# The rwkv solves split by heads, one of the two within the keys' stage; earlier S5 loads; four gate blocks ahead of glu

## The chip, the cores and the metric

One core of one Trainium2 chip runs the program in one launch. The metric is the device time of one execution in microseconds (us); lower is better. All arithmetic is float32 in effect: each dense product is made of three matmuls of split operands (below).

## What is computed

One layer over 512 latent tokens x (width 1024) with a prefix ctx of 256 tokens, cut here to what matters:

```python
x = half_ffn(x, ...); ctx = half_ffn(ctx, ...)          # SwiGLU, 1024 -> 2816 -> 1024
proj = modulate(x) @ w_in                                # u | r k v | wd ad | gd | gate_a gate_b
ya = s5_scan forward + backward + s5_D * u               # 32 groups, 64 complex states, sequential in time
r, k, v = centred_conv(proj[r k v])                      # 3x3 depthwise over 8 rows of 64 tokens
yb = rwkv_scan forward + backward                        # 8 heads of 64, a state S of 64x64 per head:
#   sa = S @ aa;  S = S * w + outer(sa, bb) + outer(v, k);  y = S @ r
ya = gelu(ya); ya = ya * sigmoid(ya @ s5_w_glu)          # "glu"
yb = (groupnorm(yb) + bonus) * g @ rwkv_w_o              # "wo"
merged = sigmoid(gate_a) * (ya @ s5_w_proj) + sigmoid(gate_b) * yb
x = x + mod * (merged @ w_out); x = half_ffn(x, ...); return rmsnorm(x)
```

The scans of ctx come first and give the start states of those of x.

## The kernel before

**Dense work.** The weights are read in pieces of 512 KB (`raw`). ScalarE rounds each to `wh`, and VectorE or GpSimd (POOL) takes the rest `wl = raw - wh`; the activations are split likewise (`hx_109`, `hx_110` are the high and low part of x's). A product takes three matmuls for each tile: wh with high, wh with low, wl with high. A piece of `w_in` makes one or two blocks of 128 output channels by 512 tokens, 24 matmuls of 512 columns a block. The list `items` (in `build`, L400) names all dense work in order: the first FFNs, `w_in` for ctx and for x, `post_items` (L1916: glu, wo, proj, w_out), the second FFN. One generator, `dense` (L353), works it off. An item may carry names of events that it has to wait for.

**How the order is set.** A planner in Python (`Plan`, L53) runs while the program is written. Each piece of work is a generator that yields what it needs next (tiles, names of events, times); `run` (L165) takes the one of the lowest priority number whose needs are ready by the planner's own clock (`RATE`, `LAT`), and so fixes the order of the instructions on each engine. On the chip each engine, and SyncE's (SP's) queue of DMA issues, works strictly in that order and waits on semaphores.

**The keys' stage.** Beside the blocks of `w_in` for x (in the order wd, ad, k0 v0 r0 to k3 v3 r3, u0 to u3, gd, the 16 gate blocks) run `pb`, `pn`, `pa`, `conv` and `v_rows`. For each of four groups of key channels VectorE does the convolution (`cvk`, `cvr`, nine-tap products), a scan over the decays (`s`), and the products `kk`, `nb`, `ep`, `ks`, `st`, which end in `abk` (DMAs of `st`) and in `lf`: the triangular 32x32 matrices of each chunk of time, head and direction, written to DRAM (`pb`, L1430). `s5_in` (L1777) makes the inputs of the S5 scan from `u` and from `gt` tiles of `GTd`, 16 pairs, loaded one ahead; `s5_rec` (L1810) then does 63 steps of the S5 recurrence on POOL (`t`, `hs`).

**The solves.** `rw_solve(n)` (L1565) inverts the triangular matrices, 128 at a time, one on each partition. VectorE does 31 steps of a product (`prod`) and a sum (`Tl`) over a rectangle of (s + 1) x (31 - s), so 62 instructions; before them `AT` is read from `lf`, POOL writes the identity into `Tl` (affine_select), and behind them `Tl` and its transpose (`Tr`, by ScalarE) go to DRAM as `ti`. The eight heads come in four pairs j, as the groups of keys do. n = 0 is for ctx, chunks 0 to 3; n = 1 takes all heads of chunks 4 to 7 and n = 2 those of chunks 8 to 11, both in the next stage.

**Stage b2** (`phase_b2`, L1882). `rw_main` (L1704, priority 0) does the steps 4 to 11 of the rwkv scan, one for each chunk of time: PE products of `T` (read from `ti`), `M`, `Z` and `AB`; the last product of a step is b<-AB,Z. `rw_pre` (1) prepares the tiles, `solves` (1) does the two solves, `s5_out` (S5O = 2, L1830) waits for the event "s5recx", loads the first tiles and makes the outputs of the S5 scan in eight pieces (16 products U,Tz and 64 hs,gt each), `s5_post` (L2034) turns them into `yg`, and `rw_post(0)` finishes half 0 of the tokens. The gd and gate blocks (hx) fill PE between, a quota of columns at a time. `phase_c` (L2115) then does `rw_post(1)`, wo, proj, w_out and the second FFN. With `GLUP = 4` the two items of glu stand four gate blocks before the last of the gates.

Of the kernel before, what the change touches and what calls it, by code (L numbers as in the profile page):

```python
# [8 lines left out]
F32 = mybir.dt.float32  # L9
F32R = mybir.dt.float32r  # L10
AF = mybir.ActivationFunctionType
OP = mybir.AluOpType
# [31 lines left out]
GLUP = 4  # L44
# [240 lines left out]
class Kern:  # L285
# [114 lines left out]
    def build(self):  # L400
# [54 lines left out]
        self.items[i] += (["b2"],)  # L455
        self.n_post = len(self.items)
# [3 lines left out]
        self.w_slots(self.W, 2, 2)  # L460
        self.alt, self.dbanks = 0, (0, 5, 7)
        self.dn = self.dense()
        with ExitStack() as pb:
            hp = pb.enter_context(self.pool("hp"))
            X.h = self.hx = [hp.tile([128, KT, NX], F32R, name=f"hx{i}") for i in range(2)]
            self.bp = pb.enter_context(self.pool("bp", side="right"))
            bcs, self.bc = self.right("bc")
            self.phase_a()
            self.dbanks = (0, 5)
            self.s5s = ExitStack()  # L470
            X.sp = self.s5s.enter_context(self.pool("s5p"))
            X.hs = X.sp.tile([128, 65, 2, 32], F32, name="hs")
            sch = self.sch
            with self.pool("q") as X.q:
                self.phase_b1(X)
                sch.add(self.s5_in(X), 3)
                sch.add(self.s5_rec(X), 2)
                sch.run(self.ctxg, self.fill, *[sch.add(g(X), p) for p, g in self.b1_gens])
            self.wms.close()
            sch.run(sch.add(self.w_retire(self.wx), 0))  # L480
            self.wxs.close()
            bcs.close()
            self.dbanks = (0, 5)
# [946 lines left out]
    def pb(self, r):  # L1430
# [5 lines left out]
        for j in range(4):  # L1436
# [6 lines left out]
            for d in range(2):  # L1443
# [105 lines left out]
    def rw_setup(self, pool):  # L1549
# [13 lines left out]
        self.rwd, self.Ls = {}, {}  # L1563

    def rw_solve(self, n, sl):  # L1565

        nc = self.nc
        V, A_ = nc.vector, nc.scalar
        ti = self.dr.tile([2, 128, 32, 32], F32, name=f"ti{n}")
        tags = dict(tag="M", bufs=2) if n == 0 else {}  # L1570
        AT = sl.tile([128, 32, 32], F32, name="AT", **tags)
        nc.sync.dma_start(AT, self.lf[4 * n:4 * n + 4].rearrange("i c (a s) t -> (i c a) s t", s=32))
        Tt = sl.tile([128, 32, 32], F32, name="Tl", **tags)
        nc.gpsimd.affine_select(Tt, self.ones[:, 0:32][:, :, None].to_broadcast([128, 32, 32]),
                                pattern=[[1, 32], [-1, 32]], base=0, channel_multiplier=0,
                                compare_op=OP.is_equal, fill=0.0)
        yield [AT, Tt]
        pr = sl.tile([128, 32, 32], F32, name="prod", tag="bt" if n == 0 else "prod", bufs=2 if n == 0 else 1)
        w = 0
        for s in range(31):  # L1580
            o = (slice(None), slice(0, s + 1), slice(s + 1, 32))
            shape = [128, s + 1, 31 - s]
            V.tensor_mul(pr[o], Tt[:, :s + 1, s:s + 1].to_broadcast(shape), AT[:, s:s + 1, s + 1:32].to_broadcast(shape))
            V.tensor_add(Tt[o], Tt[o], pr[o])
# [7 lines left out]
        nc.sync.dma_start(ti[0], Tt)  # L1592
        nc.sync.dma_start(ti[1], Tr)
        for i in range(4):
            self.rwd[4 * n + i] = (ti, i)
        self.sch.post(f"solve{n}")
# [180 lines left out]
    def s5_in(self, r):  # L1777
# [10 lines left out]
        U, gts = self.s5_u(r, 0), [load(0)]  # L1788
        for t in range(4):
            Un = self.s5_u(r, t + 1) if t < 3 else None  # L1790
            for e in range(4):
                pr = t * 4 + e
                gt = gts.pop(0)
                if pr + 1 < 16:
                    gts.append(load(pr + 1))
# [34 lines left out]
    def s5_out(self):  # L1830
        nc, X, rw = self.nc, self.X, self.X.sp
        PE, A_ = nc.tensor, nc.scalar
        yield ["s5recx"]
# [12 lines left out]
        nxt, hts = load_t(0), [load(i) for i in range(HB - 2)]  # L1846
        for t in range(4):
# [34 lines left out]
    def phase_b2(self, pb):  # L1882
# [11 lines left out]
        def solves():  # L1894
            for n in (1, 2):
                yield from self.rw_solve(n, sv)
# [314 lines left out]
```

## Time and profile before

| what | value |
|---|---|
| runs | 1859.21, 1853.49, 1851.22 us; median 1853.49 |
| profiled execution, its own time | 1853.32 us |
| its span from first to last instruction | 1851.6 us |
| TensorE (PE) busy | 1688.9 us, 91% |
| VectorE (DVE) busy | 975.9 us, 53% |
| ScalarE (ACT) busy | 718.6 us, 39% |
| GpSimd (POOL) busy | 637.0 us, 34% |
| chain that ended last | PE 68%, DMA 10%, DVE 9%, ACT 5% |

The shares are means over stages with different limits. In the rows further down, a row of the timeline gives start, duration, engine, operation, output <- inputs, sizes and count, and in brackets the idle time before it with what ended that; the name of a tile stands without its buffer number. Nearly every instruction is issued in one helper, so that L210 stands for all of them, and the tiles' names tell them apart.

### The profile page before, as it was taken

The page shows a single profiled execution, that of the slowest core. Times are in us where ns is not written, and L with a number is a line of the kernel's source. Part 1 is how long each engine was busy: PE and PEld are TensorE (multiplying, and loading weights), DVE is VectorE, ACT ScalarE, POOL GpSimd, SP SyncE. Part 2 cuts the span into 40 slices and gives each one's busy share as a digit, 9 for nine tenths or more (in the row PEclk, how much of TensorE's full clock was granted, in tenths as well). Part 3 has the DMA queues.
Part 4 walks back from the last instruction along what each step waited for, and adds up shares of the span by engine and source line. Part 5 has one row for each costly group of instructions (what it writes and reads, how often), then busy time and mean ns, then how long its engine had stood idle before and what let it go on. Part 6 is the DMA issues. An engine that isn't in the chain of part 4 may idle for free.

```text
span 1851.6 us, 33250 instructions
## 1 busy us (share of the span) xinstructions
PE 1688.9 (91%) x13280; PEld 1402.9 (76%) x13280; DVE 975.9 (53%) x1733; ACT 718.6 (39%) x1200; POOL 637.0 (34%) x815
## 2 busy tenths in 40 slices
PE   7999999899899979978999889969799999999996
PEld 3699987778787857866557567758689988888886
DVE  3486564755666645554567655743366623323335
ACT  3355442444553214534444424443543432222221
POOL 0144231556676625621112127930124421111111
PEclk9999999999999989987989979989899999999998
DMA  8955541335355556434663666456464222332321
GB/s 327 344 171 194 186 148 59 115 113 163 106 145 159 155 160 192 132 114 137 208 205 111 193 201 191 141 158 181 147 213 149 69 92 91 102 102 91 103 91 58
DMA packets 207979, 278.44 MB, mean 150 GB/s; under 512 B 93617, under 2 KB 149937, under 8 KB 206801
## 3 DMA queue, kind: packets, MB, share of 16 engines
q1 hardware_dynamic: 207824, 276.32, 48.1%
q8 instruction: 105, 1.72, 0.4%
q14 instruction: 50, 0.40, 0.1%
HBM read 234.31 MB, written 43.22 MB: 150 GB/s over the span
## 4 chain that ended last, share of the span: by engine, by line
PE 68%; DMA 10%; DVE 9%; ACT 5%; issue 3%; POOL 3%; SPq 2%; DVEq 0%; ACTq 0%; POOLq 0%
PE b L210 68%; DMA wmod<-in_wmod 2%; SPq L210 2%; DMA raw<-in_win 2%; ACT wh L210 2%; DVE wl L210 1%; POOL t L210 1%; DMA gt<-GTd 1%; DVE rs L210 1%; DMA raw<-in_wgu 1%; DMA abk<-st 1%; DVE st L210 1%; DMA gt<-gates 1%; DMA AB<-abk 1%; ACT L210 1%
## 5 line engine op out<-in xcount | busy, mean ns | idle before, releaser
L210 PE MATMUL b<-hx,wh 128*128 128x512 f32 (+1 forms) x2432 | 698.5, 374 | 27.8 <-DVE x L210 12.4
L210 POOL TENSOR_TENSOR wl<-raw,wh 128x1024 fp32r<-128x1024 f32 x109 | 265.6, 2438 | 807.1 <-ACT wh L210 744.6
L210 PEld LDWEIGHTS b<-hx,wh 128*128 128x128 f32 x2432 | 437.0, 194 | 109.6 <-ACT wh L210 24.8
L210 PE MATMUL b<-hx,wl 128*128 128x512 f32 (+1 forms) x1216 | 447.8, 368 | 8.7 <-POOL wl L210 7.6
L210 DVE TENSOR_TENSOR wl<-raw,wh 128x1024 fp32r<-128x1024 f32 x164 | 226.9, 1384 | 293.8 <-ACT wh L210 291.2
L210 ACT CAST wh<-raw 128x1024 fp32r<-128x1024 f32 x273 | 283.1, 1046 | 195.7 <-DMA raw<-in_wgu 63.3
L210 PEld LDWEIGHTS b<-hx,wl 128*128 128x128 f32 x1216 | 235.0, 193 | 49.1 <-POOL wl L210 10.5
L210 PE MATMUL b<-ah,wh 128*128 128x512 f32 (+1 forms) x560 | 196.6, 351 | 2.4 <-ACT wh L210 1.5
L210 PE MATMUL b<-ah,wl 128*128 128x512 f32 (+1 forms) x560 | 194.2, 347 | 2.5 <-POOL wl L210 1.9
L210 PE MATMUL b<-al,wh 128*128 128x512 f32 (+1 forms) x560 | 194.3, 347 | 0.1
L210 PE MATMUL b<-hc,wh 128*128 128x256 f32 x928 | 173.2, 288 | 2.0 <-ACT hc L210 1.2
L210 PEld LDWEIGHTS b<-hc,wh 128*128 128x128 f32 x928 | 145.9, 193 | 13.1 <-issue 9.5
L210 PE MATMUL b<-hc,wl 128*128 128x256 f32 x464 | 131.5, 283 | 0.0
L210 PEld LDWEIGHTS b<-ah,wl 128*128 128x128 f32 x560 | 107.0, 191 | 16.2 <-POOL wl L210 2.1
L210 PEld LDWEIGHTS b<-ah,wh 128*128 128x128 f32 x560 | 106.9, 191 | 15.8 <-ACT wh L210 1.9
L210 PEld LDWEIGHTS b<-al,wh 128*128 128x128 f32 x560 | 107.0, 191 | 12.6 <-DVE al L210 0.5
L210 ACT CAST ah<-prod 128x512 fp32r<-128x512 f32 (+1 forms) x68 | 36.6, 538 | 204.5 <-DVE prod L210 204.3
L210 DVE TENSOR_TENSOR prod<-sil,b 128x512 f32<-128x512 f32 (+1 forms) x68 | 39.6, 583 | 107.3 <-PE b L210 89.2
L210 ACT ACTIVATE sil<-b 128x512 f32<-128x512 f32 (+1 forms) x68 | 35.0, 515 | 148.5 <-PE b L210 148.4
L210 PEld LDWEIGHTS b<-hc,wl 128*128 128x128 f32 x464 | 89.2, 192 | 0.0
L210 DVE SCALAR_TENSOR_TENSOR x1c<-b,gp,x1c 128x512 f32<-128x512 f32 (+1 forms) x67 | 43.9, 662 | 74.4 <-PE b L210 74.4
L210 DVE TENSOR_TENSOR al<-prod,ah 128x512 fp32r<-128x512 f32 (+1 forms) x68 | 43.1, 633 | 41.9 <-ACT ah L210 41.9
(297 smaller groups left out, 2327.9 us busy)
## 6 DMA issues: line engine op xcount, KB each, us to landing
raw<-in_wgu SPq DMA_DIRECT2D x132, 512.0 KB, 3.6
wmod<-in_wmod SPq DMA_DIRECT2D x72, 512.0 KB, 4.9
raw<-in_wdn SPq DMA_DIRECT2D x66, 512.0 KB, 3.7
raw<-in_win SPq DMA_DIRECT2D x49, 512.0 KB, 4.1
gt<-GTd SPq DMA_DIRECT2D x32, 256.0 KB, 3.6
abk<-st SPq DMA_DIRECT2D x8, 1024.0 KB, 6.1
AB<-abk SPq DMA_DIRECT2D x8, 1024.0 KB, 6.8
GTd<-gst SPq DMA_DIRECT2D x16, 256.0 KB, 2.4
```

The source lines that it names most:

```text
L210: r = f(out, *args, **kw)
```

## The change

1. `rw_solve(1)` now takes the pairs of heads j = 0 and 1 of all chunks 4 to 11, and runs as a generator `rw_early` (priority 3) within the keys' stage, as soon as "gp2" and "lfx3" (the fourth `lf` of x written) are there; `rw_solve(2)` takes the pairs 2 and 3 of the same chunks, in b2, once "lfx7" is there. Both write one `ti`, and "solve1" and "solve2" are posted after the second. `AT` is read, and `ti` written, by two DMAs each in place of one.
2. The identity is written by two memsets of VectorE in place of POOL's affine_select; `prod` is packed (128x256).
3. `s5_in` loads its `gt` three pairs ahead in place of one; `s5_out` issues its first loads (Tz, U, two gt of Hd) once "s5inx" and "b2" are there, ahead of its wait for "s5recx".
4. `GLUP = 0` puts the two glu items behind all gate blocks, and the fourth gate block from the end waits for the event "step11", which `rw_main` posts behind its last step.

```diff
-GLUP = 4
+GLUP = 0
...
         self.items[i] += (["b2"],)
+        self.items[-4] += (["step11"],)
...
-                sch.run(self.ctxg, self.fill, *[sch.add(g(X), p) for p, g in self.b1_gens])
+                early = sch.add(self.rw_early(), 3)
+                sch.run(self.ctxg, self.fill, early, *[sch.add(g(X), p) for p, g in self.b1_gens])
...
                 nc.sync.dma_start(self.lf[ps, d * 4 + j].rearrange("s p t -> p s t"), a1)
+                self.sch.post(f"lf{e_}{i}")
...
-        ti = self.dr.tile([2, 128, 32, 32], F32, name=f"ti{n}")
+        if n < 2:
+            self.ti = self.dr.tile([2, 32 * (4 if n == 0 else 8), 32, 32], F32, name=f"ti{n}")
+        ti = self.ti
+        def rows(t, d):
+            return t.rearrange("(i d j r) s t -> d i (j r) (s t)", d=2, j=4, r=4)[d, :, 8 * n - 8:8 * n]
...
-        nc.sync.dma_start(AT, self.lf[4 * n:4 * n + 4].rearrange("i c (a s) t -> (i c a) s t", s=32))
+        if n == 0:
+            nc.sync.dma_start(AT, self.lf[0:4].rearrange("i c (a s) t -> (i c a) s t", s=32))
+        for d in range(2 if n else 0):
+            nc.sync.dma_start(AT[d * 64:d * 64 + 64].rearrange("p s t -> p (s t)"),
+                              rows(self.lf[4:12].rearrange("i c (a s) t -> (i c a) s t", s=32), d))
...
-        nc.gpsimd.affine_select(Tt, self.ones[:, 0:32][:, :, None].to_broadcast([128, 32, 32]),
-                                pattern=[[1, 32], [-1, 32]], base=0, channel_multiplier=0,
-                                compare_op=OP.is_equal, fill=0.0)
+        V.memset(Tt, 0.0)
+        V.memset(Tt.rearrange("p a b -> p (a b)")[:, ::33], 1.0)
...
-        nc.sync.dma_start(ti[0], Tt)
-        nc.sync.dma_start(ti[1], Tr)
-        for i in range(4):
-            self.rwd[4 * n + i] = (ti, i)
-        self.sch.post(f"solve{n}")
+        for k, t in enumerate((Tt, Tr)):
+            if n == 0:
+                nc.sync.dma_start(ti[k], t)
+            for d in range(2 if n else 0):
+                nc.sync.dma_start(rows(ti[k], d), t[d * 64:d * 64 + 64].rearrange("p s t -> p (s t)"))
+        for p in {0: range(4), 1: (), 2: range(4, 12)}[n]:
+            self.rwd[p] = (ti, p % 4 if n == 0 else p - 4)
+            self.sch.post(f"solve{p // 4}")
+
+    def rw_early(self):
+        yield ["gp2", "lfx3"]
+        self.wms.close()
+        es, sl = self.right("sva")
+        yield from self.rw_solve(1, sl)
+        es.close()
...
-        U, gts = self.s5_u(r, 0), [load(0)]
+        ahead = 1 if r.v else HB - 1
+        U, gts = self.s5_u(r, 0), [load(i) for i in range(ahead)]
...
-        yield ["s5recx"]
+        yield ["s5inx", "b2"]
...
         nxt, hts = load_t(0), [load(i) for i in range(HB - 2)]
+        yield ["s5recx"]
...
-            for n in (1, 2):
-                yield from self.rw_solve(n, sv)
+            yield ["lfx7"]
+            yield from self.rw_solve(2, sv)
```

**VectorE in the keys' stage.** Before, behind the product `ks` and the scan `s` of the second group of keys, stand one weight split and then the convolution of the third (the nine taps `cvk`):

```order
L210 TENSOR_TENSOR ks<-cvv,b_10225 128x512
L210 SCALAR_TENSOR_TENSOR s_9125<-m_982,s_9125 128x520
L210 TENSOR_TENSOR wl<-raw,wh 128x1024
L210 SCALAR_TENSOR_TENSOR cvk<-pad_9121,cw,cvk 128x7x63
L210 SCALAR_TENSOR_TENSOR cvk<-pad_9121,cw,cvk 128x8x63 x2
```

In the changed kernel the early solve stands there, behind the same two:

```order
L210 TENSOR_TENSOR ks<-cvv,b_10237 128x512
L210 SCALAR_TENSOR_TENSOR s_9126<-m_982,s_9126 128x520
L210 TENSOR_TENSOR prod<-Tl,AT 128x31
L210 TENSOR_TENSOR Tl<-Tl,prod 128x31
L210 TENSOR_TENSOR prod<-Tl,AT 128x60
L210 TENSOR_TENSOR Tl<-Tl,prod 128x2x30
L210 TENSOR_TENSOR wl<-raw,wh 128x1024
L210 TENSOR_TENSOR prod<-Tl,AT 128x87
```

and after its 62 instructions, with that one weight split among them, the rest of the same convolution:

```order
L210 TENSOR_TENSOR prod<-Tl,AT 128x60
L210 TENSOR_TENSOR Tl<-Tl,prod 128x30x2
L210 TENSOR_TENSOR prod<-Tl,AT 128x31
L210 TENSOR_TENSOR Tl<-Tl,prod 128x31
L210 SCALAR_TENSOR_TENSOR cvk<-pad_9122,cw,cvk 128x7x63
L210 SCALAR_TENSOR_TENSOR cvk<-pad_9122,cw,cvk 128x8x63 x2
```

The third group's convolution (all but two of its `cvk`), and all that VectorE does for the third and fourth group behind it, now follows a whole solve; two further weight splits of that stretch stand on POOL.

**PE behind step 11.** Before, the last S5 output piece is still to come behind step 11, then the transposes of `s5_post` (ident,sg), two products of the g gate, and glu (yg), whose first rows are these:

```order
L210 MATMUL b_14036<-hs,gt 64x64
L210 MATMUL b_14080<-ident,sg_13978 128x128 x4
L210 MATMUL b_14103<-sgd,g_10991 128x256 x2
L210 MATMUL b_14155<-yg_14097,wh 128x512
L210 MATMUL b_14155<-yg_14098,wh 128x512
L210 MATMUL b_14155<-yg_14097,wl 128x512
```

In the changed kernel the last S5 piece stands ahead of step 11's last products, and gate blocks (hx) follow them:

```order
L210 MATMUL b_14007<-hs,gt 64x64
L210 MATMUL b_14051<-M,Z_13626 64x64 x16
L210 MATMUL b_14051<-AB,Z_13625 64x64 x16
L210 MATMUL b_14092<-hx_109,wh 128x512
L210 MATMUL b_14092<-hx_110,wh 128x512
L210 MATMUL b_14092<-hx_109,wl 128x512
```

96 matmuls of gate blocks stand now between step 11 and glu, and none between glu and wo; two of the eight S5 pieces have moved from behind step 11 to before its end. Between the ends of steps 4 and 11 there are 96 dense matmuls where there were 123.

**SP at the S5 loads of the x stage.** Before:

```order
L210 DMA udx<-gst 128x8x64
L210 DMA U<-udx 128x512
L210 DMA gt<-GTd 128x512
L210 DMA U<-udx 128x512
L210 DMA gt<-GTd 128x512
L210 DMA abk<-st 128x8x256
L210 DMA lf<-a_10835 128x8x32
```

and in the changed kernel:

```order
L210 DMA udx<-gst 128x8x64
L210 DMA U<-udx 128x512
L210 DMA gt<-GTd 128x512 x3
L210 DMA U<-udx 128x512
L210 DMA gt<-GTd 128x512
L210 DMA abk<-st 128x8x256
L210 DMA lf<-a_10921 128x8x32
```

Two more `gt` loads of 256 KB stand ahead of an `abk` and an `lf` of the fourth group of keys.

## Rows read from the trace of the kernel before

**Rows 1.** Windows: us, busy of each engine (x instructions), granted PE clock, DMA share, GB/s.
```profile
985.00:1054.00 69.00, 67.98 (x438) 49.15 (x439) 53.68 (x88) 31.10 (x46) 12.82 (x13) 1.00 0.46 130
994.00:1076.00 82.00, 68.65 (x594) 50.98 (x593) 57.32 (x93) 33.29 (x55) 14.33 (x19) 0.91 0.54 158
1140.00:1214.00 74.00, 69.63 (x1167) 56.08 (x1165) 50.31 (x91) 34.82 (x66) 67.01 (x180) 1.00 0.55 153
1214.00:1240.00 26.00, 11.97 (x233) 10.68 (x232) 9.02 (x22) 8.63 (x15) 4.58 (x13) 0.67 0.60 177
```

**Rows 2.** Waits of PE from 1054 to 1415: total us, times, longest us.
```profile
PE b L210 <- DMA T<-ti: 13.4, 2, 12.3
PE b L210 <- DMA gt<-GTd: 12.1, 5, 5.2
PE b L210 <- ACT yg L210: 7.8, 2, 7.1
```

**Rows 3.** Waits of DVE from 994 to 1076, by the same columns.
```profile
DVE st L210 <- DMA abk<-st: 6.1, 1, 6.1
...
DVE rs L210 <- PE b L210: 3.3, 2, 2.2
DVE nb L210 <- DMA bond<-ks: 2.0, 1, 2.0
```

**Rows 4.** DVE timeline: keys' stage, and two rows in the solve for ctx.
```profile
699.91 2.47 DVE L210 TENSOR_TENSOR Tl<-Tl,prod 128x252 f32<-128x252 f32 x1
702.41 0.42 DVE L210 TENSOR_TENSOR prod<-Tl,AT 128x247 f32<-128x247 f32 x1
...
988.40 1.23 DVE L210 TENSOR_TENSOR wl<-raw,wh 128x1024 fp32r<-128x1024 f32 x1 [0.97 <-ACT wh L210]
989.55 4.38 DVE L210 SCALAR_TENSOR_TENSOR cvk<-pad,cw,cvk 128x441 f32<-128x441 f32 x6
...
1075.27 0.69 DVE L210 TENSOR_TENSOR ks<-cvv,b 128x512 f32<-128x512 f32 x1 [4.67 <-PE b L210]
```

**Rows 5.** The fourth lf of x in SP's timeline; then all lf and AT DMAs.
```profile
978.90 0.36 SPq L210 DMA_DIRECT2D lf<-a  x1
DMA to landing us min/median/max: 1.8/4.7/9.0
```

**Rows 6.** Groups of DVE, three solves together: busy us, mean ns, idle before.
```profile
L210 DVE TENSOR_TENSOR Tl<-Tl,prod 128x31 f32<-128x31 f32 (+15 forms) x93 | 36.8, 396 | 3.2
L210 DVE TENSOR_TENSOR prod<-Tl,AT 128x31 f32<-128x31 f32 (+15 forms) x93 | 34.9, 376 | 2.8
```

**Rows 7.** PE timeline: first product of steps 4 and 8, last of step 11.
```profile
1139.83 0.89 PE L210 MATMUL b<-T,M 32*32 32x32 f32 x32
1226.36 0.28 PE L210 MATMUL b<-T,M 32*32 32x32 f32 x2 [12.33 <-DMA T<-ti]
1292.54 1.15 PE L210 MATMUL b<-AB,Z 64*64 64x64 f32 x32
```

**Rows 8.** PE timeline behind step 11: last S5 piece, glu, gate blocks, wo.
```profile
1301.17 0.69 PE L210 MATMUL b<-U,Tz 128*64 128x64 f32 x16 [0.78 <-DVE y L210]
1301.79 2.51 PE L210 MATMUL b<-hs,gt 64*64 64x64 f32 x64
1313.51 1.58 PE L210 MATMUL b<-yg,wh 128*128 128x512 f32 x2 [7.11 <-ACT yg L210]
1330.46 1.03 PE L210 MATMUL b<-sgd,g 128*128 128x256 f32 x4
1332.86 0.81 PE L210 MATMUL b<-hx,wh 128*128 128x512 f32 x2
1356.32 0.61 PE L210 MATMUL b<-hx,wh 128*128 128x512 f32 x2
1357.00 0.61 PE L210 MATMUL b<-hx,wh 128*128 128x512 f32 x2
1357.69 1.89 PE L210 MATMUL b<-sgd,g 128*128 128x256 f32 x8
1359.23 0.59 PE L210 MATMUL b<-yb,wh 128*128 128x256 f32 x2
```

**Rows 9.** POOL: the S5 recurrence (ns min/median/max, first and last start us); the affine_select.
```profile
L210 POOL TENSOR_TENSOR t<-t,hs x63: 312/322/1362, 1105.8 to 1218.4; 128x64 f32<-128x64 f32 x63
1133.92 1.26 POOL L210 TENSOR_SCALAR_AFFINE_SELECT Tl<-ones 128x1024 f32<-128x1024 f32 x1 [6.33 <-DMA ti<-Tl]
```

More of the change, by code (lines that the diff above doesn't have):

```diff
@@ L460, in build @@
         self.w_slots(self.W, 2, 2)
+        self.rwd = {}
         self.alt, self.dbanks = 0, (0, 5, 7)
@@ L1562, in rw_setup @@
                 nc.gpsimd.memset(t[q * 64 + 32:q * 64 + 64, :, 0:32], 0.0)
-        self.rwd, self.Ls = {}, {}
+        self.Ls = {}
     def rw_solve(self, n, sl):
@@ L1568, in rw_solve @@
         V, A_ = nc.vector, nc.scalar
-        ti = self.dr.tile([2, 128, 32, 32], F32, name=f"ti{n}")
+        if n < 2:
+            self.ti = self.dr.tile([2, 32 * (4 if n == 0 else 8), 32, 32], F32, name=f"ti{n}")
+        ti = self.ti
         tags = dict(tag="M", bufs=2) if n == 0 else {}
+        def rows(t, d):
+            return t.rearrange("(i d j r) s t -> d i (j r) (s t)", d=2, j=4, r=4)[d, :, 8 * n - 8:8 * n]
         AT = sl.tile([128, 32, 32], F32, name="AT", **tags)
-        nc.sync.dma_start(AT, self.lf[4 * n:4 * n + 4].rearrange("i c (a s) t -> (i c a) s t", s=32))
+        if n == 0:
[3 more added lines that the diff above has]
+                              rows(self.lf[4:12].rearrange("i c (a s) t -> (i c a) s t", s=32), d))
         Tt = sl.tile([128, 32, 32], F32, name="Tl", **tags)
-        nc.gpsimd.affine_select(Tt, self.ones[:, 0:32][:, :, None].to_broadcast([128, 32, 32]),
-                                pattern=[[1, 32], [-1, 32]], base=0, channel_multiplier=0,
-                                compare_op=OP.is_equal, fill=0.0)
+        V.memset(Tt, 0.0)
+        V.memset(Tt.rearrange("p a b -> p (a b)")[:, ::33], 1.0)
         yield [AT, Tt]
-        pr = sl.tile([128, 32, 32], F32, name="prod", tag="bt" if n == 0 else "prod", bufs=2 if n == 0 else 1)
+        pr = sl.tile([128, 256], F32, name="prod", **(dict(tag="w") if n == 0 else {}))
         w = 0
@@ L1582, in rw_solve @@
             shape = [128, s + 1, 31 - s]
-            V.tensor_mul(pr[o], Tt[:, :s + 1, s:s + 1].to_broadcast(shape), AT[:, s:s + 1, s + 1:32].to_broadcast(shape))
-            V.tensor_add(Tt[o], Tt[o], pr[o])
+            q = pr[:, :(s + 1) * (31 - s)].rearrange("p (a b) -> p a b", b=31 - s)
+            V.tensor_mul(q, Tt[:, :s + 1, s:s + 1].to_broadcast(shape), AT[:, s:s + 1, s + 1:32].to_broadcast(shape))
+            V.tensor_add(Tt[o], Tt[o], q)
             w += 400 + 2.1 * (s + 1) * (31 - s)
@@ L1793, in s5_in @@
                 gt = gts.pop(0)
-                if pr + 1 < 16:
-                    gts.append(load(pr + 1))
+                if pr + ahead < 16:
+                    gts.append(load(pr + ahead))
                 yield [U, gt]
```

## The prediction

> **What bounds the kernel now.** I read the busy shares by stage first, then the waits of PE, then the timelines at the places that the change touches. Over the span PE is busy 91% of the time, so a gain can come only from stretches in which PE waits or is clocked down. In the keys' stage PE is full: 67.98 of 69 us at the full clock [rows 1]. Its last dense block ends shortly before 1054, and then PE waits for what VectorE (DVE) still has to do for the last group of keys: the stage ends with `ks` at 1075.27 [rows 4]. So from 994 on DVE's chain sets the end of that stage, though DVE is busy only 57.32 of the 82 us up to 1076 [rows 1]. In b2 PE is again nearly full from 1140 to 1214, the steps 4 to 7, and then stops once for 12.3 us, for the second solve's `T` [rows 2, 7]; behind that stop the granted clock averages 0.67 from 1214 to 1240 [rows 1]. Behind step 11 it stops for 7.1 us for `yg` [rows 2, 8].
>
> **The sum, against the profiled execution's 1853.3 us.** The median of the runs is 0.2 us from that, so the two need no correction.
>
> *1. The early solve on DVE: +21.* The three solves together take 36.8 + 34.9 us busy and 6.0 idle between their instructions [rows 6], so one takes 25.9. Its input is the fourth `lf`, issued at 978.90; that and the reading of `AT` take about 4.7 us each to land [rows 5], so the solve starts at about 988.3, where DVE has just become free. One weight split stands in it (1.23, [rows 4]), and two stand on POOL meanwhile. While POOL worked, one `Tl` of the ctx solve took 2.47 us where its neighbour took 0.42 [rows 4], so I add 2 x 2.05. Then follow the third group's taps, 4.38 [rows 4]. Together 988.3 + 25.9 + 1.2 + 4.1 + 4.4 = 1023.9, where the taps ended at 993.93 before: the chain of the last two groups starts 30 us later. Of the 82 us to the end of the stage DVE idled 24.7 [rows 1]. 10.8 of these are the round trips at its very end, 6.1 for `abk` and 4.67 for PE [rows 3, 4], and stay. The other 13.9 can take up delay at most, so the stage ends between 16 and 30 us later. Of them 5.3 are waits that the chain brings with it (`rs` 3.3, `nb` 2.0, [rows 3]); I take the remaining 8.6 as absorbed, which gives 21. The packed `prod` and the memsets change nothing that a row shows; the memsets stand in front of the solve, while it waits for `AT`. SP's queue stands behind the `lf` until `AT` may be read, some 4.7 us; the weight pieces behind it are loaded ahead and cover that, and if they did not, PE would lose up to those 4.7 us, which lies within the bounds here.
>
> *2. Clock in the keys' stage: +2 (0 to 8).* PE now waits longer for DVE. The nearest row is that of 1214 to 1240: an average of 0.67 means some 17 of 26 us at 1.2 GHz [rows 1], and the wait itself covers up to 12.3 of them. So the work loses from 2.4 us, where the low clock covers the whole wait, to 8, where it covers none; some of it falls on work that waits for DVE anyway, so 2.
>
> *3. The `gt` loads of `s5_in`, three ahead: 0 (-12.1 to +2).* PE waited 12.1 us for them in five waits [rows 2], all beside the DVE chain that ends the stage, which now is longer still: the cover grows. Two loads more stand ahead of `abk` and `lf` on SP. The bound of -12.1 holds only where DVE isn't last, which the term before excludes; +2 is two more issues and their share of the traffic.
>
> *4. From the start of b2 to step 4: +1 (0 to 5).* One solve of the same size still stands there, with `AT` and `ti` in two DMAs each; its Tl identity leaves POOL.
>
> *5. Steps 4 to 11: -17.* They take from 1139.83 to 1293.69, or 153.9 us [rows 7]. Step 8 no longer waits for `T`: -13.4 in two waits [rows 2]. The low clock behind the stop goes too: between 2.4 and 8 as above, 4 taken. 27 fewer dense matmuls stand between: three take 0.68 us (from 1356.32 to 1357.00, [rows 8]), so -6.1. Two S5 pieces more stand there, each from 1301.17 to 1304.30, so 3.1 [rows 8]: +6.2. Bounds -8 (another wait keeps half) to -22.
>
> *6. From step 11 to wo and behind: -18.* The two S5 pieces leave (-6.2). 96 gate matmuls now stand over the chain that makes `yg`, 7.8 us of waits [rows 2]: -7.8. Glu ran from 1313.51 to 1330.46, 17 us, for 48 matmuls that take 10.9 at the full clock: -6. The gate blocks behind it ran 24.8 us (1332.86 to 1357.69, [rows 8]) where the full clock gives 21.8: -3. Against that, nothing now covers the chain behind glu and `rw_post` for wo: between nothing and another 7.1, the wait for `yg`, which is a chain of the same make; 5 taken. Bounds -13 to -24.
>
> Sum: +21 + 2 + 0 + 1 - 17 - 18 = -11, which gives 1853.3 - 11 = **1842**.
>
> **The rivals.**
>
> *A. The steps are not shortened, because the S5 recurrence on POOL comes late.* In the new order a piece of S5 output stands before the end of step 8, and PE waits in order. The recurrence starts when `s5_in` is done: 1105.8 before, some 21 later now, and took 113 us to 1218.8 [rows 9]. Without the affine_select and the wait for it (1.26 + 6.33, [rows 9]) it takes 105.4 and ends at about 1232. Step 8 begins at 1139.83 + 24 + 74 = 1238. The margin is 6 us. For it: POOL was 67 of 74 us busy in b2 [rows 1]. Against it: 250 operations of 0.32 us need only 81 us [rows 9], and the rest of the 113 is waiting, part of it beside a solve that is gone. If the recurrence is 17 us late, PE loses the 11 beyond the margin: 1842 + 11 = **1853**. Chance 0.22.
>
> *B. The delay is absorbed.* The planner may have used the 13.9 us of DVE's idle time wholly, and POOL may not hold the solve: 30 - 13.9 - 4.1 = 12, and no clock loss: 1842 - 9 - 2 = **1831**. Chance 0.12.
>
> *C. Slower: PE loses its clock in the keys' stage itself.* The products that need the third group's taps stand among dense blocks that PE does in order. If PE gets there before DVE, it stops within the dense work, not behind it, and then runs its dense matmuls at 1.2 GHz. In the 69 us of rows 1 PE ran at 2.4 GHz without a gap; 32 us of that work at half clock cost 32 us more, and the DVE chain does not hide this, since the last group's taps wait for those blocks. It decides from the point where the stage's delay exceeds 21 + 11 + 9 = 41 us; with 32 of loss, of which 3 are already counted, the time is 1842 + 29 = **1871**. For it: the drop to 0.67 behind one stop of 12.3 us. Against it: dense blocks stand between the solve and those products (some 40 to 53 dense matmuls were moved in ahead of them, 9 to 12 us). The Trainium skill ("TensorE: Matmul & The Clock Gate", Part 1: The HAM clock gate) calls the throttled clock the default state, which activity releases; by that rule a stop in mid-stage would bring 1.2 GHz with it, as in C, and the trace agrees, with 0.67 behind the stop. Chance 0.09.
>
> *D. The early solve is not early.* If its `AT` landed only with the last `lf`, both solves would follow each other in b2 and step 4 would wait for both: the 12.3 us stop returns ahead of step 4, and only term 6 is left: 1853 - 18 + 12 = 1847. The `lf` at 978.90 speaks against it. Chance 0.05.
>
> **How the numbers follow.** The forecast has 0.52, and its own range is 1829 to 1853, from the bounds: the keys' stage 5 less or 9 more, terms 5 and 6 some 9 either way, not all at once. Rival B lies in it, and A just at its end; C lies outside. 0.08 is left out on the slow side and some 0.1 below 1827, so the range is 1827 to 1857. A measurement of this kernel tells 0.5%, 9.3 us, from no change: faster is below 1844.2, slower above 1862.8. Faster: 0.41 of the forecast's 0.52, 0.12 of B, and 0.02 of D: 0.55. Slower: C's 0.09. The rest, 0.36, is within.
>
> **What would show it.** Right: 62 solve instructions on DVE from about 988 to 1018; the stage's last `ks` at about 1096; no wait of PE for `ti` behind step 4's; steps 4 to 11 in about 137 us at a clock of 1.00; no wait of over 2 us for `yg`; glu in 11 us; a new wait of some 5 us ahead of wo. Wrong: a PE wait for `hs` or Hd within steps 8 to 11 (A); a last `ks` before 1088 (B); a granted clock well under 1.00 before the last dense block of the keys' stage (C); the gain of term 6 eaten by a wait for `yb` of over 10 us.

## The result, and the profile after

Median of the changed kernel 1868.2 us (1862.0 to 1872.5), of the kernel before, measured beside it, 1855.7; ratio 1.0067, 95% interval 1.0038 to 1.0096. It is about 12 us slower where 11 us faster were forecast, and outside the range of 1827 to 1857. The profiled execution took 1870.22 us, with a span of 1868.4. From the page: the busy row of PE and the chain that ended last, by engine.

```profile
PE 1699.7 (91%) x13280; PEld 1416.2 (76%) x13280; DVE 974.1 (52%) x1735; ACT 721.0 (39%) x1202; POOL 642.7 (34%) x816
...
PE 61%; DVE 12%; DMA 11%; ACT 5%; POOL 5%; issue 4%; SPq 2%; DVEq 0%; ACTq 0%; POOLq 0%
```

PE's share of the chain falls from 68% to 61%, and what waits on DVE, DMA and POOL takes its place. The windows, by the columns of [rows 1], for the keys' stage, two stretches of the steps and the stretch from step 11 to w_out; the second and third hold earlier steps than in [rows 1], as step 4 now begins 31 us later:

```profile
985.00:1054.00 69.00, 53.86 (x313) 36.78 (x312) 58.44 (x118) 23.27 (x34) 12.58 (x9) 0.88 0.30 94
1140.00:1214.00 74.00, 68.34 (x708) 54.28 (x706) 32.88 (x54) 28.93 (x47) 66.95 (x180) 0.95 0.52 148
1214.00:1240.00 26.00, 23.65 (x466) 20.00 (x466) 9.97 (x16) 13.07 (x27) 12.57 (x43) 1.00 0.61 159
1319.50:1429.70 110.20, 95.04 (x580) 84.69 (x581) 64.82 (x104) 53.95 (x77) 37.21 (x16) 0.95 0.62 199
```

The stretch from step 11 to w_out in the kernel before:

```profile
1293.70:1414.40 120.70, 105.72 (x760) 93.34 (x761) 69.89 (x119) 54.33 (x83) 30.21 (x13) 0.90 0.59 191
```

In the keys' stage PE is busy 53.86 of 69 us where it was 67.98 [rows 1], at a clock of 0.88 instead of 1.00. The DVE timeline there, answering to [rows 4]:

```profile
988.90 0.19 DVE L210 TENSOR_TENSOR prod<-Tl,AT 128x31 f32<-128x31 f32 x1 [0.75 <-DMA AT<-lf]
...
1001.59 2.48 DVE L210 TENSOR_TENSOR Tl<-Tl,prod 128x256 f32<-128x256 f32 x1
...
1015.10 0.21 DVE L210 TENSOR_TENSOR Tl<-Tl,prod 128x31 f32<-128x31 f32 x1
1015.22 4.38 DVE L210 SCALAR_TENSOR_TENSOR cvk<-pad,cw,cvk 128x441 f32<-128x441 f32 x6
...
1093.53 0.69 DVE L210 TENSOR_TENSOR st<-kk,ep 128x512 f32<-128x512 f32 x1 [10.25 <-DMA abk<-st]
...
1101.79 0.69 DVE L210 TENSOR_TENSOR ks<-cvv,b 128x512 f32<-128x512 f32 x1 [1.93 <-PE b L210]
```

The solve runs from 988.90 to 1015.3, one `Tl` in it takes 2.48 us instead of 0.42, beside the only weight split that POOL does in that time (1001.25 to 1003.79), the taps start 25.7 us later than before, and the stage's last `ks` comes 26.5 later. PE, answering to [rows 7, 8]:

```profile
1022.47 1.87 PE L210 MATMUL b<-blk,sqk 128*128 128x2 f32 x8 [12.58 <-ACT sqk L210]
...
1170.93 0.31 PE L210 MATMUL b<-T,M 32*32 32x32 f32 x2 [2.88 <-DMA T<-ti]
1172.42 1.06 PE L210 MATMUL b<-T,M 32*32 32x32 f32 x30 [1.19 <-DMA T<-ti]
...
1243.28 0.69 PE L210 MATMUL b<-T,M 32*32 32x32 f32 x32
...
1318.35 1.15 PE L210 MATMUL b<-AB,Z 64*64 64x64 f32 x32
...
1333.74 0.73 PE L210 MATMUL b<-hx,wh 128*128 128x512 f32 x2 [1.77 <-ACT wh L210]
1336.17 0.50 PE L210 MATMUL b<-hx,wl 128*128 128x512 f32 x1 [1.70 <-POOL wl L210]
...
1347.60 0.73 PE L210 MATMUL b<-yg,wh 128*128 128x512 f32 x2 [0.70 <-ACT wh L210]
1350.04 0.51 PE L210 MATMUL b<-yg,wl 128*128 128x512 f32 x1 [1.71 <-POOL wl L210]
...
1367.63 0.38 PE L210 MATMUL b<-yb,wh 128*128 128x256 f32 x1 [4.12 <-ACT yb L210]
...
1429.71 0.47 PE L210 MATMUL b<-hx,wh 128*128 128x256 f32 x2
```

The 12.3 us stop at step 8 is gone (1243.28, its first product, has no wait), and so is the one for `yg`. New are a stop of 12.58 in mid-stage, for the third group's `sqk`, 4.1 for step 4's `T`, waits for `wh` and `wl` around glu, and 4.12 for `yb`.

To compare runs I cut each trace at six landmarks: the issue of the fourth `lf`, the end of the last `ks`, the first T,M of step 4, the end of step 11's AB,Z, the first w_out matmul, the end of the span. The lengths in us:

| run | lf to ks | ks to step 4 | steps 4 to 11 | step 11 to w_out | w_out to end | ratio to before |
|---|---|---|---|---|---|---|
| before | 97.1 | 63.9 | 153.9 | 120.7 | 437.2 | 1 |
| n1_null | 96.7 | 62.6 | 152.9 | 121.3 | 435.9 | 0.9990 |
| n2_dram | 98.5 | 62.7 | 153.0 | 119.6 | 434.5 | 0.9999 |
| changed | 122.9 | 68.5 | 148.6 | 110.2 | 438.7 | 1.0067 |
| e1_gates | 97.6 | 61.0 | 154.3 | 127.3 | 436.2 | 1.0094 |
| e2_s5loads | 98.6 | 64.9 | 152.6 | 121.0 | 438.1 | 1.0040 |
| e3_early | 120.7 | 67.7 | 149.4 | 107.8 | 436.7 | 1.0081 |
| e5_no_early_split | 98.3 | 64.5 | 177.5 | 102.0 | 436.6 | 1.0071 |
| e4_early_last | 121.0 | 69.3 | 146.8 | 109.5 | 440.4 | 1.0072 |
| e6_no_gates | 121.6 | 68.8 | 147.4 | 108.3 | 435.5 | 1.0030 |
| e8_prefetch | 119.5 | 69.8 | 146.3 | 109.9 | 439.4 | 1.0054 |
| e10_half | 106.8 | 71.8 | 142.5 | 108.3 | 439.1 | 0.9986 |
| e11_lfx5 | 132.0 | 71.5 | 161.0 | 106.9 | 434.1 | 1.0193 |
| e12_own_buffers | 97.3 | 64.7 | 150.2 | 120.8 | 435.9 | 0.9989 |
| e13_glup2 | 120.4 | 68.9 | 148.9 | 109.1 | 439.4 | 1.0044 |
| e14_pool | 128.8 | 68.9 | 175.1 | 90.9 | 438.8 | 1.0159 |
| e15_glup2_alone | 97.0 | 63.0 | 151.3 | 121.6 | 441.1 | 1.0018 |

The ratio comes from the medians of all runs, the lengths from one profiled execution each. The fourth `lf` itself lies at 977 to 993 us in these executions, and at 978.9 and 983.8 in two with the same instructions, so lengths are compared and not places. The two with the same instructions, before and n1_null, agree to 1.3 us in every column, and n2_dram's to 2.7; a difference of that size in one column shows nothing.

### The profile page after: what moved, and what is told of

It is laid out like the page before. It is cut to its first block, busy times and chain, and to the rows that moved or that the text cites. A ratio compares the mean times of both kernels' runs of the same rounds, so it can differ in the third digit from the quotient of the medians.

```text
span 1868.4 us, 33259 instructions
## 1 busy us (share of the span) xinstructions
PE 1699.7 (91%) x13280; PEld 1416.2 (76%) x13280; DVE 974.1 (52%) x1735; ACT 721.0 (39%) x1202; POOL 642.7 (34%) x816
## 4 chain that ended last, share of the span: by engine, by line
PE 61%; DVE 12%; DMA 11%; ACT 5%; POOL 5%; issue 4%; SPq 2%; DVEq 0%; ACTq 0%; POOLq 0%
PE b L210 61%; POOL t L210 3%; DMA wmod<-in_wmod 2%; SPq L210 2%; ACT wh L210 2%; DMA gt<-GTd 2%; DVE wl L210 1%; DVE st L210 1%; DMA AB<-abk 1%; DVE Tl L210 1%; DVE prod L210 1%; POOL hs L210 1%; DMA abk<-st 1%; DMA raw<-in_win 1%; POOL wl L210 1%
## 5 line engine op out<-in xcount | busy, mean ns | idle before, releaser
L210 POOL TENSOR_TENSOR wl<-raw,wh 128x1024 fp32r<-128x1024 f32 x113 | 276.0, 2443 | 814.3 <-ACT wh L210 779.4
L210 PEld LDWEIGHTS b<-hx,wh 128*128 128x128 f32 x2432 | 442.2, 196 | 100.4 <-ACT wh L210 15.1
L210 DVE TENSOR_TENSOR wl<-raw,wh 128x1024 fp32r<-128x1024 f32 x160 | 216.5, 1354 | 289.5 <-ACT wh L210 283.9
L210 PE MATMUL b<-hc,wh 128*128 128x256 f32 x928 | 177.4, 292 | 2.7 <-ACT hc L210 1.2
```

The source lines that it names most:

```text
L210: r = f(out, *args, **kw)
```

## The experiments

**The parts alone.** After the result my theory was that the early solve loses and the gate move gains. e1_gates is the kernel before with part 4 alone:

```diff
-GLUP = 4
+GLUP = 0
+        self.items[-4] += (["step11"],)
```

> The kernel before with part 4 alone (GLUP = 0, the fourth gate block from the end waits for step 11). Theory (the loss of the change is the early solve, the gate move gains): from the end of step 11 to the first w_out matmul 120.7 us become about 111, as in the changed kernel (110.2), and the time is 8 to 10 us below before, ratio about 0.995. Rival (the gate move itself takes back what it gives, by new waits for weight splits and by rw_post products with no dense work beside them): that stretch stays at 118 or more and the ratio is 1.000 or above.

Measured 1.0094 (1.0058 to 1.0130); from step 11 to w_out 127.3 us. The theory fell. PE's waits in that stretch (us in total, times, longest), where before had 14.9 in all, 7.8 of them for `yg` [rows 2], and this run has 20.6; the first three:

```profile
PE b L210 <- ACT yb L210: 10.3, 1, 10.3
PE b L210 <- ACT wh L210: 5.4, 3, 3.3
PE b L210 <- POOL wl L210: 1.7, 1, 1.7
```

The trace was 9 us behind at the fourth `lf`, ahead of any moved instruction, so the +6.6 of that stretch is the surer measure of the part; what made the rest of the 1.0094 is open.

e2_s5loads, part 3 alone:

```diff
-        U, gts = self.s5_u(r, 0), [load(0)]
+        ahead = 1 if r.v else HB - 1
+        U, gts = self.s5_u(r, 0), [load(i) for i in range(ahead)]
...
-        yield ["s5recx"]
+        yield ["s5inx", "b2"]
...
+        yield ["s5recx"]
```

> The kernel before with part 3 alone (gt of s5_in three ahead, first loads of s5_out ahead of its wait). Theory: the waits for gt, 12.1 us in the kernel before, lie beside DVE's chain, so the last ks moves by less than 2 us and the time stays within 3 us of before (ratio 0.998 to 1.002). Rival: the loads delay abk and lf on the queue, so that the last ks comes 4 us or more later and the ratio is 1.002 to 1.005; or the waits were on the path, and the ratio is about 0.994.

Measured 1.0040 (1.0015 to 1.0065). The last `ks` moved by 1.6 us, as the theory has it, and no other stage by more than 1.3; but the ratio is the rival's. The stages behind the fourth `lf` sum to +2.5: the loads give nothing, and a few us may be lost, not located.

e3_early is the changed kernel without parts 3 and 4:

```diff
-GLUP = 0
+GLUP = 4
-        self.items[-4] += (["step11"],)
-        ahead = 1 if r.v else HB - 1
+        ahead = 1
...
-        yield ["s5inx", "b2"]
+        yield ["s5recx"]
...
-        yield ["s5recx"]
```

> The kernel before with parts 1 and 2 alone (solves split by heads, the first in the keys' stage, identity by memset). Theory: the keys' stage ends about 26 us later, 13 come back at step 8, and the time is 15 to 25 us above before, ratio 1.008 to 1.013, so more than the whole change's 1.0067. Rival (the gate move is the loss): the ratio is 1.003 or less.

Measured 1.0081 (1.0051 to 1.0112): keys' stage +23.6, from there to step 4 +3.8, steps -4.5, from step 11 to w_out -12.9. The ratio is at the lower end of the theory's; the gate move is not the whole loss. e5_no_early_split is the kernel before with parts 3 and 4, so with the edits of e1 and e2.

> The changed kernel without parts 1 and 2: parts 3 and 4 on the kernel before. Theory: the gain of the gate move stands alone, ratio 0.993 to 0.997, the best so far; the 12.3 us wait for the second solve's T is back. Rival (the gate move is the loss): ratio 1.000 or above.

Measured 1.0071 (1.0040 to 1.0102). Here all eight S5 pieces stand ahead of step 11's end, so the two columns have to be taken together: 279.5 us, against 274.6 before. So each large part loses alone. They lose less together than summed: in e3, e6 and the changed kernel all eight pieces stand ahead of step 11's end as well, and the stretch behind it is short (108 to 110 us) whether part 4 is there or not.

**A control.** Since all four came out slower, n1_null adds three empty lines to the source of the kernel before, and n2_dram declares its buffer `x1d` last:

```diff
-        self.x1d = D_("x1d", 128, KT, NX)
...
         self.yd = D_("yd", 4, 128, 8, 64)
+        self.x1d = D_("x1d", 128, KT, NX)
```

> The kernel before with three empty lines in its source, so that every engine has the same instructions in the same order: a control for what the comparison itself does. Theory (the parts' losses are made by the parts): ratio 1.000, its interval holding 1. Rival (building the program anew, with nothing changed, costs some us by itself, since gates alone came out 15 us slow while its trace was 9 us behind at the fourth lf, ahead of its first moved instruction): ratio 1.004 to 1.009.

Measured 0.9990 (0.9969 to 1.0012).

> The kernel before with one DRAM buffer (x1d) declared last instead of first, so that the buffers' addresses in DRAM shift and no instruction moves. Theory: ratio 1.000, within 0.002. Rival (addresses matter): a ratio of 1.004 or more, with the time lost ahead of the fourth lf.

Measured 0.9999 (0.9979 to 1.0019). Neither a new build nor the addresses in DRAM cost more than some 0.2%.

**The early solve.** e4_early_last puts its stream behind the others:

```diff
-                early = sch.add(self.rw_early(), 3)
+                early = sch.add(self.rw_early(), 8)
```

> The changed kernel with the early solve's stream at priority 8 instead of 3, so that its instructions stand among those of the third group of keys instead of ahead of them. Theory (the solve ahead of the third group's taps stops PE for 12.6 us and delays the chain): that stop of PE shrinks to under 6 us, the last ks comes 5 to 12 us earlier against the fourth lf than in the changed kernel, and the ratio to before is 0.998 to 1.003. Rival (DVE's total work sets the stage's end, wherever the solve stands): last ks within 3 us of the changed kernel's, ratio about 1.007.

Measured 1.0072 (1.0052 to 1.0093); the stage takes 121.0 us, 1.9 less than in the changed kernel. PE's 12.6 us stop for `sqk` shrank to 5.4, as the theory has it, but a stop of 13.4 for `st` took its place, and both the stage and the ratio are the rival's. e10_half leaves out half of the solve:

```diff
-        for s in range(31):
+        for s in range(0, 31, 1 if n != 1 else 2):
```

> The changed kernel with every second of the 31 steps of the early solve left out (its heads get another result), so about 12 us less of DVE in the keys' stage. Theory (the stage is later by what the early solve takes on DVE): from the fourth lf to the last ks 111 us instead of 122.9, PE's stop of 12.6 us under 3, ratio to before 0.999 to 1.002. Rival (the place and the new order make the delay, not the amount): 119 us or more, ratio above 1.004.

Measured 0.9986 (0.9961 to 1.0012); the stage takes 106.8 us, still less than the theory's 111, and PE waits there no longer for `sqk`, but 6.5 us for `st`. With none, half and all of the early solve on DVE the stage takes 97 to 99, 106.8 and 120 to 123 us, and e4 shows that the place within it matters little: the amount of DVE's work makes the delay. e11_lfx5 waits for the sixth `lf`:

```diff
-        yield ["gp2", "lfx3"]
+        yield ["gp2", "lfx5"]
```

> The changed kernel with the early solve waiting for the sixth lf of x instead of the fourth, so that the third group of keys goes ahead of it. Theory (DVE has waits of 10 us for abk and others in the last 50 us of the stage that a solve there can use): from the fourth lf to the last ks 112 to 117 us, ratio to before 1.001 to 1.004. Rival (as with priority 8: DVE's total work sets the end): 120 us or more, ratio about 1.007.

Measured 1.0193 (1.0160 to 1.0227): the stage takes 132.0 us, which is the rival's, but the ratio is worse than either has it. Against the changed kernel it loses 9.1 us in the stage, 3 from there to step 4 and 9 in the next two columns together; the last column gives 4.6 back, and the rest of the loss is not located. The solve (1065 to 1095) now stands ahead of the fourth group's last products, so that the last `st` and `abk` come later; DVE's waits for POOL's `ks` grew as well, from 1.7 to 13.2 us. Which of the two weighs more was not tried. e14_pool does the early solve on POOL, without part 4:

```diff
-GLUP = 0
+GLUP = 4
-        self.items[-4] += (["step11"],)
...
-            V.tensor_mul(q, Tt[:, :s + 1, s:s + 1].to_broadcast(shape), AT[:, s:s + 1, s + 1:32].to_broadcast(shape))
-            V.tensor_add(Tt[o], Tt[o], q)
+            E = nc.gpsimd if n == 1 else V
+            E.tensor_mul(q, Tt[:, :s + 1, s:s + 1].to_broadcast(shape), AT[:, s:s + 1, s + 1:32].to_broadcast(shape))
+            E.tensor_add(Tt[o], Tt[o], q)
...
-                yield [("V", 800)]
+                yield [("P" if n == 1 else "V", 800)]
```

> The changed kernel without part 4 and with the early solve's products and sums on POOL, which was busy 12.8 of 69 us in that stage, instead of on DVE. Theory (the stage is later by what the early solve takes of DVE): from the fourth lf to the last ks 97 to 108 us instead of 121.6, the gain at step 8 stays, ratio to before 0.993 to 0.999. Rival (POOL's instructions hold up DVE's two-input ones as they did in the solve for ctx, 2.47 us instead of 0.42, or the order the planner makes of it is no better): 115 us or more, ratio 1.001 or above.

Measured 1.0159 (1.0126 to 1.0192), stage 128.8 us. The groups of POOL from 970 to 1110 (busy us, mean ns):

```profile
L210 POOL TENSOR_TENSOR Tl<-Tl,prod 128x31 f32<-128x31 f32 (+15 forms) x31 | 23.2, 748 | 2.4
L210 POOL TENSOR_TENSOR prod<-Tl,AT 128x31 f32<-128x31 f32 (+15 forms) x31 | 22.1, 714 | 6.5 <-DVE s L210 4.4
```

45 us against DVE's 24, and DVE then waited 8.9 us for `ks`, which POOL makes behind it. Its longest wait in total is another:

```profile
DVE wl L210 <- ACT wh L210: 24.3, 7, 7.0
```

The kernel before has 7.0 us of it up to its last `ks`. So taking the solve off DVE did not shorten the stage: against the kernel before DVE is busy there for 10 us more (76.4 us; one tap took 2.71 us instead of 0.68) and idle for 22 more (52.3). What made its weight splits wait is open. Nor did the gain at step 8 stay: the stop for `T` is gone, but glu now stands ahead of step 11's end, and the two columns together are 266.0 us against 255.8 in e6, its like with the solve on DVE. The figures are the rival's, but that POOL's instructions hold up DVE's is the smaller part of it.

**The gate move.** e6_no_gates takes part 4 out of the changed kernel:

```diff
-GLUP = 0
+GLUP = 4
-        self.items[-4] += (["step11"],)
```

> The changed kernel without part 4 (GLUP = 4, no wait for step 11). Theory, formed after gates alone came out slower (from step 11 to w_out 127.3 us there, 120.7 before): part 4 costs about 6 us, so this is 6 us faster than the changed kernel, ratio to before about 1.003. Rival (in the changed kernel part 4 gains, since the S5 pieces are out of the way: 110.2 us against 120.7): about 6 to 10 us slower than the changed kernel, ratio 1.010 to 1.012.

Measured 1.0030 (1.0012 to 1.0049), against 1.0067 with part 4. The ratio is the theory's and not the rival's, but the two intervals overlap, and from step 11 to w_out the two differ by 1.9 us only: part 4 doesn't gain here, and that it loses 6 is not shown. PE's waits from step 11 to w_out, all three that there are, and then the first four of the changed kernel:

```profile
PE b L210 <- ACT yg L210: 6.1, 2, 5.6
PE b L210 <- DVE gb L210: 5.8, 2, 4.8
PE b L210 <- ACT wh L210: 0.7, 1, 0.7
```

```profile
PE b L210 <- ACT yb L210: 4.1, 1, 4.1
PE b L210 <- ACT wh L210: 3.6, 3, 1.8
PE b L210 <- POOL wl L210: 3.4, 2, 1.7
PE b L210 <- DVE gb L210: 2.0, 2, 1.0
```

The wait for `yg` goes, and waits for `yb` and for weights come: 12.6 us become 15.0 in all, with PE busy for 95.5 and 95.0 us at a mean clock of 0.92 and 0.95. e8_prefetch asks whether the wait for step 11 holds back the weights, by setting it behind the prefetch in `dense`:

```diff
-            if len(self.items[i]) > 4:
-                yield self.items[i][4]
+            need = self.items[i][4] if len(self.items[i]) > 4 else None
+            if need and need != ["step11"]:
+                yield need
...
+            if need == ["step11"]:
+                yield need
```

> The changed kernel, with the dense stream's wait for step 11 put behind its loads and splits of the next weight pieces instead of ahead of them. Theory (the wait for step 11 also holds back the weight pieces behind it, hence PE's 7.0 us of waits for wh and wl between step 11 and w_out): these waits fall under 2.5 us, that stretch takes about 105 us instead of 110.2, ratio to before 1.003 to 1.005. Rival (the splits are late because ACT and SP do gelu, its table loads and the yd round trips first): the waits stay at 5 us or more and the ratio at about 1.007.

Measured 1.0054 (1.0029 to 1.0080), 109.9 us, and 5.7 us of waits for `wh` and `wl`: nearer the rival. All waits fell from 15.0 to 11.5 us, but PE was busy for 98.2 us instead of 95.0, at a clock of 0.91 instead of 0.95, so that the stretch is as long as it was. ACT's timeline in the changed kernel shows the rival's work:

```profile
1330.23 0.62 ACT L210 CAST yg<-ga 128x512 fp32r<-128x512 f32 x1
1330.87 1.28 ACT L210 ACT_TABLE_LOAD   x1
1332.16 0.60 ACT L210 ACTIVATE gst<-b 128x512 f32<-128x512 f32 x1
1332.66 1.04 ACT L210 CAST wh<-raw 128x1024 fp32r<-128x1024 f32 x1
1333.71 1.28 ACT L210 ACT_TABLE_LOAD   x1
1335.00 1.18 ACT L210 ACTIVATE ga<-yi 128x384 f32<-128x384 f32 x2
```

Gate blocks (`gst`) and the gelu (`ga`) now alternate, with a table load at each turn (four around that stretch, where the kernel before has two), and the casts of the next weights queue behind both; PE's wait at 1333.74 ends with that cast. e13_glup2 leaves two of the four blocks behind glu:

```diff
-GLUP = 0
+GLUP = 2
```

> The changed kernel with GLUP = 2 instead of 0: of the four gate blocks that wait for step 11, two stand ahead of glu and two behind it. Theory (part 4 lost because nothing covers the chain from glu to yb, whose buffers glu frees, and the weight pieces that come late): the 4.1 us wait for yb goes, PE's waits from step 11 to w_out sum to 8 us or less instead of 15, that stretch takes 103 to 106 us instead of 110.2, ratio to before 1.002 to 1.005. Rival (yg's chain then has too little cover, and the waits only move back to yg): 109 us or more, ratio about 1.007.

Measured 1.0044 (1.0027 to 1.0061), 109.1 us: the rival's time, by another way.

```profile
PE b L210 <- DVE gb L210: 6.1, 4, 3.1
PE b L210 <- POOL wl L210: 3.4, 2, 1.7
PE b L210 <- ACT wh L210: 2.3, 2, 1.8
PE b L210 <- ACT sg L210: 2.0, 1, 2.0
```

The wait for `yb` is gone, and the waits still come to 13.8 us in all. e15_glup2_alone is the same on the kernel before:

```diff
-GLUP = 4
+GLUP = 2
+        self.items[-4] += (["step11"],)
```

> The kernel before with GLUP = 2 and the wait for step 11 alone: two gate blocks ahead of glu, two behind, the solves as before. Theory (two blocks, 11 us, cover the chain to yg, two the chain to yb): from step 11 to w_out 112 to 117 us instead of 120.7 (before) or 127.3 (GLUP = 0), ratio 0.995 to 0.998. Rival (the weight pieces come late whatever the split, 5 to 7 us): 120 us or more, ratio 1.000 to 1.004.

Measured 1.0018 (0.9996 to 1.0040), 121.6 us from step 11 to w_out: no gain either. The time is the rival's, but not its reason, as PE waited only 1.1 us for weights there. Its longest wait stands ahead of glu's first product and ends 0.7 us after DVE's second `yg`; the trace names no releaser ("issue"):

```profile
PE b L210 <- issue: 8.3, 1, 8.3
```

So two gate blocks did not cover the chain to `yg`.

**A try at the same stop by another way.** e12_own_buffers leaves the solves where they were and loads the second one's `AT` with the first's:

```diff
...
+        AT = self.AT2 if n == 2 else load(n)
+        if n == 1:
+            self.AT2 = load(2)
...
```

> The kernel before, its two solves by chunks and both in b2 as they were, but the second solve's AT in a buffer of its own and loaded together with the first's, the identity by memset and prod packed: the second solve no longer waits for the first one's ti to land, POOL's affine_select and AT's trip. Theory (the 12.3 us stop at step 8 comes from solve 2 starting at 1145.6, 15 us after solve 1 ends): it starts 8 to 10 us earlier, the stop falls to 2 to 5 us, steps 4 to 11 take 145 us instead of 153, ratio to before 0.994 to 0.997, the best of all. Rival (solve 2 is paced by the steps' own DVE work and by POOL, 74 us for 24 us of work): it ends at most 3 us earlier, ratio 0.998 to 1.000.

Measured 0.9989 (0.9963 to 1.0014). Against step 4's start solve 2 begins 7.7 us earlier, but ends only 3.9 earlier, and the stop at step 8 is still 10.3 us: nearer the rival. In the 74 us of solve 2 in the kernel before, DVE waited 14.5 us for `wh`, with the solve queued behind the weight splits; that this order on DVE paces the solve is likely, and wasn't tried. No whole version beat the kernel before beyond its interval.

## Why the prediction was wrong

Of the signs that the prediction named, most came true: the solve on DVE from 988.9 to 1015.3, no wait for `ti` behind step 4's, no long wait for `yg`, glu at the full clock, a wait of 4.1 us ahead of wo. The last `ks` came at 1101.79 instead of 1096, and the steps took 148.6 us instead of 137. Such signs say that each mechanism was there, and not what it was worth. Against the prediction's own terms, in us (measured as differences of the lengths above):

| term | predicted | measured |
|---|---|---|
| 1, 2 and 3: keys' stage | +23 | +25.8 |
| 4: to step 4 | +1 | +4.6 |
| 5: steps 4 to 11 | -17 | -5.3 |
| 6: step 11 to w_out | -18 | -10.5 |
| behind w_out | 0 | +1.5 |

With 0.7 at the fourth `lf` that is the span's +16.8.

*Term 1* had the mechanism and the place: start at 988.3 (988.90 measured), end of the chain within its bounds. Two sizes in it were too large: one hold by POOL, of 2.06 us, stands where two were taken, and without it and the weight split the solve took 23 us where 25.9 were taken; that price was a mean over three solves, with the one for ctx and its holds among them. What failed is "I take the remaining 8.6 as absorbed": 25.7 at the taps became 26.5 at the last `ks`. From the fourth `lf` to the last `ks`, before and after:

```profile
978.90:1076.00 97.10, 83.75 (x647) 60.71 (x647) 66.42 (x104) 41.12 (x66) 21.06 (x26) 0.92 0.52 153
979.60:1102.50 122.90, 92.90 (x681) 67.56 (x680) 87.65 (x166) 44.15 (x72) 26.95 (x28) 0.85 0.46 139
```

DVE is busy for 21.2 us more and idle for 35.3 us instead of 30.7. Its idle time lay in waits for PE, ACT and DMA and moved along with the chain; the wait for `abk` even grew from 6.1 to 10.25. *Rival C* named the place, a stop among the dense blocks, and the clock did fall to 0.88, but the delay stayed at 26 us, under its 41. The Trainium skill ("TensorE: Matmul & The Clock Gate", Part 1: The HAM clock gate) has the clock released by activity; the trace agrees with 0.88 in a stretch with that stop. How much of the 26 us is clock no run separates, so term 2 stays open.

*Term 4* took one solve of the same size as the same time. It began 19.7 us after `ks` (18.7 before), took 37.6 us (35.6), and step 4's first `T` product came 11.2 us behind its end (9.6), after a wait of 2.88. The doubled DMAs of `AT` and `ti` are the likely cause of part of it; that wasn't tried.

*Term 5* had four parts. Step 8 took 27.3 us and takes 14.4: the stop of 13.4 went, one S5 piece (3.1) came in, and so 2.6 are left for the clock, which was 0.73 in that step before and is 1.00 now; 4 were taken. Over all eight steps the mean clock is 0.93 before and after, where 1.00 was forecast. Steps 4 to 7 gave 1.8 us, where 27 dense matmuls fewer were credited with 6.1: 1.19 of waiting for `T` came in, and the first 12 dense matmuls behind that wait took 4.76 us instead of 3, at a clock of 0.61. And the 27 were too many: from step 4's first product to step 11's end the traces show 91 dense matmuls where there were 111, and between the ends of the two steps 60 and 77. The 20 that left, worth 4.5 us at the prediction's price, stand ahead of step 4 now. What failed most in this term is the "+6.2" for two S5 pieces, priced by their products alone: steps 9 to 11, with one piece more, took 61.8 us instead of 52.4. The products that follow the pieces in `s5_post` and `rw_post(0)` (ident,sg 1.1; blk2c,sg 1.95) came with them, and a wait of 2.0 for ACT's `ys`; some 1 us remains.

*Term 6* is the step that failed most, though the table hides it. It credited the gate move with -7.8 - 6 - 3 + 5 = -12, and the runs show no gain: PE's waits in the stretch come to 14.9 us before and 15.0 after. With the solves moved, part 4 makes the stretch 1.9 us longer (the changed kernel against e6, and 3.2 more behind it, about what two executions of one program differ by); alone, it makes it 6.6 longer (e1). The -10.5 in the table are busy time of PE, 105.7 against 95.0 us: some 9 of them are the two S5 pieces (hs,gt 5.1 and U,Tz 1.7) with the products behind them (blk2c,sg 1.9; ident,sg 0.6), which left for the steps. They leave without part 4 too (e3, 107.8).

Item by item: the windows of glu and of the gate blocks before, then those of glu and of the start of wo after (the row of glu after counts its own products alone, and has no column for POOL):

```profile
1313.50:1330.46 16.96, 16.29 (x48) 10.94 (x49) 6.88 (x9) 11.27 (x17) 2.24 (x1) 0.71 0.84 280
1332.86:1357.69 24.83, 24.83 (x123) 20.82 (x122) 14.77 (x26) 13.11 (x22) 5.29 (x3) 1.00 0.39 128
...
1347.60:1361.60 14.00, 11.61 (x48) 8.88 (x48) 0.00 (x0) 0.00 (x0) 1.00 0.88 304
1367.63:1378.46 10.83, 9.78 (x41) 8.90 (x41) 5.67 (x19) 3.08 (x5) 2.35 (x1) 0.53 0.62 194
```

The wait for `yg` went, as forecast, and glu got its clock back: 16.3 us busy at 0.71 became 11.6 at 1.00. The -3 for the gate blocks was never there: they ran at 1.00 before, and what they took beyond 21.8 us are the blk2c,sg (1.84) and ident,sg (1.03) among them. On the other side the wait for `yb`, 4.1, was in the sum (5), but the waits for weights, 7.0, were not, and neither was the clock behind the new stop: wo now begins with 10.8 us at a mean of 0.53, so nearly all at 1.2 GHz, and its blk2c,sg take 3.58 us instead of the 1.84 among the gate blocks before, and each three of its products 0.64 instead of 0.36. By these prices that costs some 4 us, about what glu gained. So covering the one stop moved the wait and the low clock to the next. e8, e13 and e15 split or feed the cover in other ways, and none makes the stretch shorter by more than the executions differ.

*Rival A* didn't happen: the recurrence began 20.7 us later and ended at 1228, ahead of step 8 and its first S5 piece (1243.3 and 1243.9). *Rivals B and D* fell with the taps at 1015.22 and the `AT` at 988.9. None of the rivals had the sum: a loss in the keys' stage nearly as forecast, under a third of the gain in the steps, and of the gate move none.

## What to carry to other kernels

Before work is moved into an engine's idle time, ask what ends each gap: gaps that end with another engine's answer can travel with the chain, and absorbed nothing here. Where a stretch is a chain of waits over several engines, covering one wait with dense work takes that cover from the next, where the stop may bring the low clock with it, and the dense work brings its own needs (casts, splits, loads, tables) into the queues of the chain; price those, and take credit for the difference only. Work that moves brings its followers: price the products and waits behind it too.

## What the runs showed of the hardware

The same 62 instructions of one solve took some 24 us on DVE and 45 us on POOL (714 and 748 ns a piece against some 376 and 396). Step 8 of the kernel before began with 8.1 us at 1.2 GHz (granted 0.50, 1226.36 to 1234.50), behind its stop; PE was busy for 6.45 of them, with four groups of small products that take 4.0 us at the full clock in step 7 of the changed kernel, so that these 8.1 us cost some 2.5. Behind the 4.12 us stop for `yb` the clock was 0.53 for 10.8 us, though PE was busy for 9.78 of them. Two builds of one program lay 5 us apart at the fourth `lf` and agreed within 1.3 us in each stage behind it, a third, with other addresses in DRAM, within 2.7.
